# Feed-forward: where the two Silus of a part stand in ScalarE's queue

## The chip, the cores and the metric

The kernel runs on one core of a Trainium2 chip. A core has TensorE (PE) for matrix products, VectorE (DVE), ScalarE (ACT) and GpSimd (POOL) for work on tiles, and SyncE (SP), whose queue issues all the DMAs here. Each engine works through its own queue of instructions in order and waits by semaphores for the others. The metric is the device time of one execution in microseconds (us). A few runs of one kernel lie within about 0.2% of each other.

## The reference

Two sequences (one of 256 positions, one of 512, handled together as T = 768 columns) go through a trunk of two layers, each with a mixer (an mLSTM in layer 0, sliding-window attention in layer 1) and a feed-forward with a convolution. The change is in the feed-forward:

```
def conv_ffn(h, w_up, conv_w, conv_b, w_down):
    u = h @ w_up                                  # 1024 -> 2 * 2816
    u = depthwise_conv_width_3(u, conv_w) + conv_b
    g = u[..., :D_FF]
    val = u[..., D_FF:]
    return (jax.nn.silu(g) * val) @ w_down        # 2816 -> 1024
```

So each gate channel goes through the convolution and a Silu, and is multiplied by its value channel, before the down projection.

## The kernel before, in words

Channels lie on the 128 partitions and positions along the free dimension. All arithmetic is fp32. To multiply at speed, every fp32 operand is split into a rounded part ("hi", a cast on ScalarE, L236) and the remainder ("lo", a subtraction on VectorE, L237), and a product is made of three matmuls: hi x hi, lo x hi, hi x lo (L1275, L1276, L1277).

The 2816 gate channels and the 2816 value channels are cut into 11 **parts** of 256 and 256 (p = 0 to 10; the loop stands at the end of `ffn`). A part has two **pairs**: pair i = 0 makes the two blocks of 128 gate channels, pair i = 1 the two blocks of 128 value channels. `up(p)` makes both, then `down(p-1)` is written, so the down projection of one part stands behind the up projection of the next.

A pair multiplies by a scheme of Strassen's kind: seven products of quarter size instead of eight, called B11, B21, T1, T2, T3, T4 and B22 in the code, each of 12 matmuls (`quarters`). They accumulate in four fixed banks of PSUM, a, e, b and d. In the order in which `pair` writes them:

- B11 into a; ScalarE copies a to b (L1319, the **first copy**, or fork);
- T1 into e; ScalarE copies e to `p5` (L1324);
- T2 into b; ScalarE copies b to d (L1330, the **second copy**);
- B21 into a; ScalarE evicts a to the output row r1 (L1283 within `evict`);
- T3 into d; ScalarE copies d to `u3` (L1338, the **third copy**);
- B22 into b; VectorE makes the second half of r1 (L1340) and of r2 (L1341);
- T4 into d; ScalarE evicts d to r2.

The weights of a pair are loaded by SP, added up on POOL (L1303, L1306, L1307, L1315) and split on ScalarE and VectorE into buffers `whi` and `wlo`, three of each; a cast waits until PE has done with the buffer that it takes.

Behind each pair `up` writes the convolution of its two rows (`conv`): one step on ScalarE (L1499) and two on VectorE (L1501, L1502). For pair 0 each convolution is followed by a Silu on ScalarE in place (L1526). For pair 1 POOL multiplies the row by the gate's row (L1528) and the product is split for the down projection.

Part 0 is special: its two pairs are written out by hand in `head`, in an order that is kept as it is written on PE, ScalarE and VectorE (`manual_schedule`), and in part 1 the first pair lacks the two products that `head` has already made (`rest`), and both pairs' instructions are tied behind the end of `head` (`issue_after`).

Elsewhere the order of each engine's queue isn't the order of the text. When the kernel is built, a planner with a model of the instructions' times (`schedule_with_timeline_sim=True`) lays the instructions out: on each engine it issues what its model holds to be ready, earlier lines of the program first. The queues are fixed from then on. `issue_after(ins)` is a constraint for this planner: the instructions that a block writes on the engine of `ins` are issued behind `ins`. It adds no wait by a semaphore.

Of the kernel before, what the change touches and what calls it, by code (L numbers as in the profile page):

```python
# [12 lines left out]
AF = mybir.ActivationFunctionType  # L13
# [65 lines left out]
def col(t):  # L79

    return t + (GAP if t >= 256 else 0)
# [64 lines left out]
class Net:  # L146
# [1148 lines left out]
    def pair(self, pool, u, bank, rows, rest=False):  # L1295


        nc = self.nc
        r1, r2 = rows
        rb, ra = (self.load(u, h) for h in (1, 0))  # L1300
        q = [t[:, 512 * i : 512 * (i + 1)] for t in (ra, rb) for i in range(2)]
        tt = nc.gpsimd.tensor_tensor
        tt(q[2], q[2], q[3], ALU.add)  # L1303
        if not rest:
            wa = self.split(ra)
        tt(q[0], q[2], q[0], ALU.subtract)  # L1306
        tt(q[1], q[1], q[0], ALU.subtract)  # L1307
        s1h, s1l = (pool.tile([P, 512], R, tag=t, name=self.nm(t), bufs=1) for t in ("s1h", "s1l"))
        part = lambda w, i: [t[:, 512 * i : 512 * (i + 1)] for t in w]
        fork = r1[:, col(H) :]  # L1310
        if not rest:
            fork = a = bank(0)
            self.quarters(a, part(wa, 0), self.B11, True)
        self.fp_copy_split(s1h, s1l, q[2])
        tt(q[2], q[3], q[0], ALU.subtract)  # L1315
        wc = self.split(ra)
        wb = self.split(rb)
        e, b = bank(1), bank(2)
        nc.scalar.copy(b, fork)  # L1319
        p5 = self.tmp([P, H])  # L1320

        def fifth():
            self.quarters(e, (s1h, s1l), self.T1, True)
            nc.scalar.copy(p5, e)  # L1324

        if not rest:
            fifth()
        self.quarters(b, part(wc, 0), self.T2, False)
        d = bank(3)
        nc.scalar.copy(d, b)  # L1330
        if rest:
            fifth()
        else:
            self.quarters(a, part(wa, 1), self.B21, False)
            self.evict(r1, a)
        self.quarters(d, part(wb, 0), self.T3, False)
        u3 = self.tmp([P, H])
        nc.scalar.copy(u3, d)  # L1338
        self.quarters(b, part(wc, 1), self.B22, False)
        nc.vector.tensor_tensor(r1[:, col(H) :], b, p5, ALU.add)  # L1340
        nc.vector.tensor_tensor(r2[:, col(H) :], e, u3, ALU.add)  # L1341
        self.quarters(d, part(wb, 1), self.T4, False)
        self.evict(r2, d)

    def prepare(self, u0, l):

        flat = [z.rearrange("p j k t -> p (j k t)") for z in (self.zh, self.zl)]
        place = lambda j: [z[:, j : j + 1024] for z in flat]

        ahead = [place(12 * H), place(4 * H)]  # L1350
        wa = place(0)
        spare = None
        if l:

            spare = self.slab([P, 3072], R)
            wa = [spare[:, 1024 * (z + 1) : 1024 * (z + 2)] for z in range(2)]
        self.fp_copy_split(*wa, self.load(u0 + 1, 0))
        for i in range(0 if l else 2):
            self.fp_copy_split(*ahead[i], self.load(u0 + 3 + i, 0))
        return wa, ahead, spare  # L1360
# [123 lines left out]
    def ffn(self, l, xt, pool, last_tile, apply, keep=None):  # L1484
        nc = self.nc
        u0 = U_FFN + l * NPART * 3
        early = self.prepare(u0, l)
        next(last_tile)

        urows = [self.slab([P, 4, TG]) for _ in range(2)]  # L1490
        for urow in urows:
            nc.gpsimd.memset(urow[:, :, 256 : 256 + GAP], 0.0)

        behind = []

        def conv(u, y, ch):
            cb = self.cst(CB + l * 44 + ch)
            w = lambda tap: self.cst(CW + (l * 44 + ch) * 3 + tap)
            nc.scalar.activation(y, u, AF.Identity, bias=cb, scale=w(1))  # L1499
            stt = nc.vector.scalar_tensor_tensor  # L1500
            stt(y[:, 1:], u[:, :-1], w(0), y[:, 1:], ALU.mult, ALU.add)  # L1501
            stt(y[:, :-1], u[:, 1:], w(2), y[:, :-1], ALU.mult, ALU.add)  # L1502

        def up(p):
            urow = urows[0] if p == 0 else urows[1]
            fixed = lambda i: self.bank[i][:, :H]
            if p == 0:
                eng = mybir.EngineType
                self.ready(HALVES[0])
                with self.tc.manual_schedule(engines={eng.PE, eng.Activation, eng.DVE}):  # L1510
                    behind[:] = self.head(u0, last_tile, pool, urows, mark, early)
            for i in range(2):
                if p:
                    rows = [urow[:, 2 * i + j] for j in range(2)]
                    with ExitStack() as order:
                        for ins in behind[2 * i :] if p == 1 else ():
                            order.enter_context(self.tc.issue_after(ins))
                        self.pair(pool, u0 + 3 * p + i, fixed, rows, rest=p == 1)
                if i == 0:
                    yrow = self.slab([P, 4, TG])  # L1520
                    g = self.slab([P, 2, 2, TG], R)
                for j in range(2):
                    y = yrow[:, 2 * i + j]
                    conv(urow[:, 2 * i + j], y, i * FC + 2 * p + j)
                    if i == 0:
                        nc.scalar.activation(y, y, AF.Silu)  # L1526
                    else:
                        nc.gpsimd.tensor_tensor(y, y, yrow[:, j], ALU.mult)  # L1528
                        self.fp_copy_split(g[:, 0, j], g[:, 1, j], y)
            return g  # L1530

        def mark(t):

            hi, _ = self.quarter(self.B11)
            self.mm(t, hi[0][:, :P], hi[0], True, True)

        def down(p, g):
            ws = (w for _, w in self.halves(u0 + 3 * p + 2))
            chunk = lambda w, i: [t[:, 512 * i : 512 * (i + 1)] for t in w]

            def tile(w, c, rng):
                s0, s1, _ = rng
                o = self.pa()[:, : s1 - s0]
                cs = slice(c % 4 * P, (c % 4 + 1) * P)
                for i in range(2):
                    wh, wl = chunk(w, i)
                    gh, gl = (g[:, z, i, col(s0) : col(s0) + s1 - s0] for z in range(2))
                    self.mm(o, wh[:, cs], gh, i == 0, False)
                    self.mm(o, wh[:, cs], gl, False, False)
                    self.mm(o, wl[:, cs], gh, False, i == 1)  # L1550
                self.resid(xt, o, l, 40, c, rng)

            if p < NPART - 1:
                for h, w in enumerate(ws):
                    for rng in SAMPLE, PROMPT:
                        for c in range(4 * h, 4 * h + 4):
                            tile(w, c, rng)
                return
            ws = list(ws)
            for rng in RANGES:  # L1560
                norm = Norm(self, xt, rng, apply, last=keep is None and rng is RANGES[-1], adds=None if keep is not None else nc.vector)
                for c in range(KC):
                    tile(ws[c // 4], c, rng)
                    norm.square(c)
                    if keep is not None or rng is not RANGES[-1] or c < 3:
                        self.tick(0.65)
                if keep is not None:
                    self.save_x(xt, keep, rng)
                self.start(rng, norm.stages())

        prev = None
        for p in range(NPART):
            g = up(p)
            if prev is not None:
                down(*prev)
            prev = (p, g)
        down(*prev)
# [175 lines left out]
```

## Time and profile before

| | |
|---|---|
| median of 3 runs | 1882.17 us (1879.48 to 1883.78) |
| the profiled execution | 1885.06 us, its span 1883.3 us |
| PE busy | 1799.4 us |
| VectorE / ScalarE / POOL busy | 1412.1 / 912.2 / 488.7 us |
| Silus (L1526) | 44, of 848 ns (median) |
| the feed-forward's parts 1 to 10 | from about 555 us in layer 0 and from about 1373 us in layer 1 |

The span runs from the first to the last instruction. A row of a timeline gives the start in us from there, the length in us, the engine, the line of the kernel, the operation with the tile that it writes and those that it reads, and in brackets how long the engine stood idle before it and what ended that. "L1526" is line 1526 of the kernel before. Matmuls overlap: each is listed with about 0.33 us, but they start about 0.175 us apart.

### The profile page before, as it was taken

What the parts mean: (1) busy time and instruction counts of PE and PEld (TensorE: products, weight loads), DVE (VectorE), ACT (ScalarE), POOL (GpSimd) and SP (SyncE); (2) the same over time, 40 slices, a digit from 0 to 9 for tenths busy, and PEclk for the clock granted to TensorE, in tenths of its full rate; (3) what the DMA queues carried; (4) which work ended last, traced back from release to release, by engine and by line L of the source; (5) the groups of instructions that cost most, each with busy time, mean ns of one, the idle gap of its engine ahead of it and who ended that gap; (6) DMA issues with size and microseconds to landing.
All of it is one profiled execution on the core that took longest, in us unless ns stands there. A gap on an engine that the chain in (4) does not pass through costs nothing. (4 is left out here: it accounts for less than half of the span.)

```text
span 1883.3 us, 29169 instructions
## 1 busy us (share of the span) xinstructions
PE 1799.4 (96%) x11306; PEld 1659.1 (88%) x11306; DVE 1412.1 (75%) x2306; ACT 912.2 (48%) x1841; POOL 488.7 (26%) x390
## 2 busy tenths in 40 slices
PE   6989999999999999999999999989999999999997
PEld 5968887889988999999999988879989999999996
DVE  5866577685699777777777768865998777777777
ACT  4544334434464444444444557764564444444443
POOL 2010001021023333333332213330134333333322
PEclk9999999999999999999999999999999999999999
DMA  8354466556212122222223221312222222222211
GB/s 323 108 163 140 153 196 206 162 177 199 79 51 68 63 68 67 67 68 68 68 68 104 81 86 47 104 43 91 68 90 67 68 68 68 68 68 68 68 34 68
DMA packets 64246, 184.49 MB, mean 98 GB/s; under 512 B 6167, under 2 KB 23831, under 8 KB 64108
## 3 DMA queue, kind: packets, MB, share of 16 engines
q1 hardware_dynamic: 64108, 182.63, 30.0%
q8 instruction: 89, 1.46, 0.3%
q14 instruction: 49, 0.40, 0.1%
HBM read 176.17 MB, written 6.43 MB: 97 GB/s over the span
## 5 line engine op out<-in xcount | busy, mean ns | idle before, releaser
L236 ACT CAST whi<-raw 128x1024 fp32r<-128x1024 f32 x237 | 249.1, 1051 | 403.4 <-PE pa L230 197.4
L237 DVE TENSOR_TENSOR wlo<-raw,whi 128x1024 fp32r<-128x1024 f32 x237 | 331.1, 1397 | 113.9 <-ACT whi L236 108.5
L230 PE MATMUL pa<-slab,whi 128*128 128x256 f32 (+1 forms) x1472 | 347.3, 333 | 4.8 <-DVE slab L719 4.6
L230 PEld LDWEIGHTS pa<-slab,whi 128*128 128x128 f32 x1472 | 253.0, 190 | 31.8 <-DVE slab L719 6.3
L719 DVE SCALAR_TENSOR_TENSOR slab<-pa,mod,slab 128x256 f32<-128x256 f32 (+1 forms) x368 | 207.8, 592 | 70.8 <-PE pa L230 70.2
L230 PE MATMUL ps<-zh,whi 128*128 128x256 f32 (+2 forms) x688 | 232.5, 339 | 6.1 <-ACT whi L236 2.6
L230 PE MATMUL pa<-slab,wlo 128*128 128x256 f32 (+1 forms) x736 | 235.2, 331 | 0.0
L230 PE MATMUL ps<-zh,wlo 128*128 128x256 f32 (+2 forms) x688 | 227.0, 332 | 3.8 <-DVE wlo L237 3.8
L230 PE MATMUL ps<-zl,whi 128*128 128x256 f32 (+2 forms) x688 | 227.9, 332 | 1.4 <-DVE zl L539 0.9
L1275 PE MATMUL ps<-zh,whi 128*128 128x384 f32 x504 | 171.2, 340 | 16.7 <-ACT ps L1330 15.2
L1276 PE MATMUL ps<-zl,whi 128*128 128x384 f32 x504 | 169.8, 337 | 0.8 <-DVE zl L1233 0.8
L1277 PE MATMUL ps<-zh,wlo 128*128 128x384 f32 x504 | 169.1, 336 | 0.0
L230 PEld LDWEIGHTS pa<-slab,wlo 128*128 128x128 f32 x736 | 139.5, 190 | 13.0 <-DVE wlo L237 0.9
L230 PEld LDWEIGHTS ps<-zh,whi 128*128 128x128 f32 x688 | 131.0, 191 | 20.0 <-issue 3.5
L230 PEld LDWEIGHTS ps<-zh,wlo 128*128 128x128 f32 x688 | 131.2, 191 | 14.8 <-DVE wlo L237 4.8
L230 PEld LDWEIGHTS ps<-zl,whi 128*128 128x128 f32 x688 | 131.3, 191 | 10.4 <-DVE zl L539 1.1
L1528 POOL TENSOR_TENSOR slab<-slab 128x772 f32<-128x772 f32 x44 | 83.8, 1906 | 210.5 <-DVE slab L1502 199.1
L1306 POOL TENSOR_TENSOR raw<-raw,raw 128x512 f32<-128x512 f32 x40 | 52.3, 1308 | 293.9 <-DVE wlo L237 243.8
L1501 DVE SCALAR_TENSOR_TENSOR slab<-slab,cstt,slab 128x771 f32<-128x771 f32 x88 | 105.7, 1202 | 27.0 <-ACT slab L1499 27.0
L1502 DVE SCALAR_TENSOR_TENSOR slab<-slab,cstt,slab 128x771 f32<-128x771 f32 x88 | 120.2, 1366 | 0.8
L1275 PEld LDWEIGHTS ps<-zh,whi 128*128 128x128 f32 x504 | 94.6, 188 | 24.8 <-ACT ps L1330 20.4
L472 DVE SCALAR_TENSOR_TENSOR ada<-raw,silc,ada 128x1024 f32<-128x1024 f32 x84 | 111.6, 1360 | 2.3 <-DMA raw<-in_adaln_w_dram 2.3
(300 smaller groups left out, 4127.9 us busy)
## 6 DMA issues: line engine op xcount, KB each, us to landing
raw<-in_w_dram SPq DMA_DIRECT2D x208, 512.0 KB, 3.7
raw<-in_adaln_w_dram SPq DMA_DIRECT2D x84, 512.0 KB, 4.5
slab<-in_x_dram SPq DMA_DIRECT2D x12, 512.0 KB, 8.9
slab<-in_adaln_w_dram SPq DMA_DIRECT2D x12, 512.0 KB, 10.2
slab<-mrows SPq DMA_DIRECT2D x8, 384.0 KB, 5.4
xs<-slab SPq DMA_DIRECT2D x6, 512.0 KB, 2.9
bt<-brow SPq DMA_DIRECT2D x16, 192.0 KB, 3.3
slab<-xs SPq DMA_DIRECT2D x6, 512.0 KB, 5.7
```

The source lines that it names most:

```text
L230: self.last_mm = self.nc.tensor.matmul(out, lhsT, rhs, start=start, stop=stop)
L236: nc.scalar.copy(hi, src)
L237: return nc.vector.tensor_tensor(lo, src, hi.bitcast(F32), ALU.subtract)
L472: stt(acc[:, s], row, w, acc[:, s], ALU.mult, ALU.add)
L719: self.nc.vector.scalar_tensor_tensor(x, o, self.mod[l][:, gc + c, q : q + 1], x, ALU.mult, ALU.add)
L1275: mm(o, wh[:, k], hi[k], start=start and k == 0, stop=False, skip_group_check=True)
L1276: mm(o, wh[:, k], lo[k], start=False, stop=False, skip_group_check=True)
L1277: mm(o, wl[:, k], hi[k], start=False, stop=k == 3, skip_group_check=True)
L1306: tt(q[0], q[2], q[0], ALU.subtract)
L1501: stt(y[:, 1:], u[:, :-1], w(0), y[:, 1:], ALU.mult, ALU.add)
L1502: stt(y[:, :-1], u[:, 1:], w(2), y[:, :-1], ALU.mult, ALU.add)
L1528: nc.gpsimd.tensor_tensor(y, y, yrow[:, j], ALU.mult)
```

## The change

The two Silus of a part are no longer written behind the convolutions of the first pair. They are written ahead of the second pair's convolutions, and, in every part but part 0, tied behind the third copy of the second pair, which `pair` now returns. Part 0, whose pairs are made in `head`, has no such copy and gets no tie.

```diff
@@ pair
         u3 = self.tmp([P, H])
-        nc.scalar.copy(u3, d)
+        third = nc.scalar.copy(u3, d)
...
         self.quarters(d, part(wb, 1), self.T4, False)
         self.evict(r2, d)
+        return third.ins
@@ ffn, up
-                        self.pair(pool, u0 + 3 * p + i, fixed, rows, rest=p == 1)
+                        third = self.pair(pool, u0 + 3 * p + i, fixed, rows, rest=p == 1)
                 if i == 0:
                     yrow = self.slab([P, 4, TG])
                     g = self.slab([P, 2, 2, TG], R)
+                if i:
+                    with self.tc.issue_after(third) if p else ExitStack():
+                        for j in range(2):
+                            nc.scalar.activation(yrow[:, j], yrow[:, j], AF.Silu)
                 for j in range(2):
                     y = yrow[:, 2 * i + j]
                     conv(urow[:, 2 * i + j], y, i * FC + 2 * p + j)
-                    if i == 0:
-                        nc.scalar.activation(y, y, AF.Silu)
-                    else:
+                    if i:
                         nc.gpsimd.tensor_tensor(y, y, yrow[:, j], ALU.mult)
                         self.fp_copy_split(g[:, 0, j], g[:, 1, j], y)
```

## The prediction

> **What bounds the kernel now.** I read the page first: busy shares, the shares of the chain that ended last, and the costliest groups.
>
> ```profile
> span 1883.3 us, 29169 instructions
> ...
> PE 1799.4 (96%) x11306; PEld 1659.1 (88%) x11306; DVE 1412.1 (75%) x2306; ACT 912.2 (48%) x1841; POOL 488.7 (26%) x390
> ...
> L1275 PE MATMUL ps<-zh,whi 128*128 128x384 f32 x504 | 171.2, 340 | 16.7 <-ACT ps L1330 15.2
> ```
>
> PE is busy for 96% of the span, so in the feed-forward only a wait of PE itself can be worth time. Of the idle time in front of the feed-forward's matmuls, 15.2 us is put down to one ScalarE instruction, the second copy of a pair (L1330, which forks bank b into bank d). Next I asked for the waits of PE alone, in two windows. The first holds parts 2 to 9 of layer 0 and the start of part 10; the second, parts 2 to 10 of layer 1 from the end of part 2's first pair.
>
> ```profile
> PE ps L1275 <- ACT ps L1330: 5.6, 7, 0.9
> PE ps L1275 <- ACT ps L1319: 0.2, 1, 0.2
> ```
> ```profile
> PE ps L1275 <- ACT ps L1330: 7.1, 7, 1.9
> PE ps L1275 <- ACT ps L1319: 0.2, 1, 0.2
> ```
>
> The columns are microseconds in total, times, and the longest. In some 780 us PE waits for hardly anything else: 7 + 7 waits of 5.6 + 7.1 = 12.7 us, one in the second pair of each of parts 3 to 9. ScalarE's timeline in part 3 (bracket: idle time before the row, and what ended it) says why.
>
> ```profile
> 665.77 0.84 ACT L1526 ACTIVATE slab<-slab 128x772 f32<-128x772 f32 x1
> ...
> 669.75 0.47 ACT L1324 COPY nt<-ps 128x384 f32<-128x384 f32 x1
> 672.03 0.85 ACT L1526 ACTIVATE slab<-slab 128x772 f32<-128x772 f32 x1 [1.80 <-DVE slab L1502]
> 672.78 0.47 ACT L1330 COPY ps<-ps 128x384 f32<-128x384 f32 x1
> 673.19 1.04 ACT L236 CAST whi<-raw 128x1024 fp32r<-128x1024 f32 x1
> ...
> 675.69 0.48 ACT L1338 COPY nt<-ps 128x384 f32<-128x384 f32 x1 [1.03 <-PE ps L1277]
> 677.64 1.06 ACT L236 CAST whi<-raw 128x1024 fp32r<-128x1024 f32 x1 [1.46 <-PE ps L1276]
> 678.59 1.03 ACT L1499 ACTIVATE slab<-slab,cstt 128x772 f32<-128x772 f32 x1
> ```
>
> The second Silu (672.03) stands in ScalarE's queue ahead of L1330. It waits 1.80 us for the convolution's last VectorE step, runs, and only then does the copy go. PE at the same place:
>
> ```profile
> 671.81 0.33 PE L1277 MATMUL ps<-zh,wlo 128*128 128x384 f32 x1
> 671.98 0.34 PE L1276 MATMUL ps<-yl,whi 128*128 128x384 f32 x1
> 672.16 0.34 PE L1277 MATMUL ps<-yh,wlo 128*128 128x384 f32 x1
> 673.30 0.44 PE L1275 MATMUL ps<-zh,whi 128*128 128x384 f32 x1 [0.81 <-ACT ps L1330]
> 673.59 0.34 PE L1276 MATMUL ps<-zl,whi 128*128 128x384 f32 x1
> ```
>
> The row at 671.81 is the last matmul of T2 into bank b, on which L1330 depends. Only two matmuls of B21 are left as filler behind it; at 673.30 T3 begins, on the copied bank.
>
> **The change part by part.** *What is removed:* in parts 3 to 9 both Silus leave the queue ahead of L1330. It does not go to nothing, because L1330 still has to follow T2's last matmul. How quickly it can is seen where no Silu stands before it, in part 10 (ScalarE, then PE):
>
> ```profile
> 1002.37 0.46 ACT L1330 COPY ps<-ps 128x384 f32<-128x384 f32 x1 [1.88 <-PE ps L1277]
> ```
> ```profile
> 1002.00 0.33 PE L1277 MATMUL ps<-zh,wlo 128*128 128x384 f32 x1
> 1002.18 0.34 PE L1276 MATMUL ps<-yl,whi 128*128 128x384 f32 x1
> ...
> 1003.41 0.34 PE L1277 MATMUL ps<-yh,wlo 128*128 128x384 f32 x1
> 1003.59 0.34 PE L1275 MATMUL ps<-zh,whi 128*128 128x384 f32 x1
> ```
>
> The copy started 1002.37 - 1002.00 = 0.37 us after the start of T2's last matmul. There eight fillers followed (1002.18 to 1003.41) and PE did not wait. In part 3 T3 started 673.30 - 672.78 = 0.52 us after the copy. So T3 can start 0.37 + 0.52 = 0.89 us after T2's last matmul starts: 671.81 + 0.89 = 672.70 instead of 673.30. That is 0.60 of the 0.81 us; 0.21 us of idle time stays, since two fillers cover too little. L1324 ends at 670.22, ahead of the new start of 672.18, so nothing on ScalarE holds the copy.
>
> The sum over 14 parts: 12.7 us less 14 x 0.21 = 2.9 leaves **9.8 us**. This takes PE's order as it is. That is my choice between two ends. If the planner leaves no filler, T3 follows T2's last matmul by 0.89 against a modelled end of 0.34: idle 0.55, sum 12.7 - 14 x 0.55 = 5.0 us. If it leaves many fillers, as in part 10, the wait goes whole, and with it the restart: from 672.16 to 673.59 is 1.43 us for two steps of 0.18, so a stall of 0.81 costs 1.07, 0.27 us more than its idle time; the sum is 12.7 + 14 x 0.27 = 16.5 us. I take the middle because the fillers are spent while T2 waits for its weights, and no Silu feeds those.
>
> The Trainium skill (TensorE: Matmul & The Clock Gate, "Single matmul latency") gives a lone warm matmul of N columns (398 + N)/2.4 ns, so 326 ns for 384. No row here shows that latency alone; with 0.33 for the 0.37 above, an estimate by the page, the residue would be 0.17 us and the sum 10.3. The same section against its back-to-back gap of N/2.4 + 2.5 ns makes a restart 0.16 us; the rows show 0.27, and by the page the whole wait would be worth 15.0 us instead of 16.5.
>
> *What is added behind the third copy (L1338):* two Silus, in all 20 parts that have a second pair.
>
> ```profile
> L1526 ACT ACTIVATE slab<-slab x44: 833/848/860, 562.4 to 1821.7; 128x772 f32<-128x772 f32 x44
> ```
>
> Start to start a Silu takes 672.78 - 672.03 = 0.75 us, two 1.50. ScalarE is idle for 1.46 us after L1338, until PE frees a buffer for the weight cast at 677.64. The pair fills that gap and delays the cast and the convolution's L1499 behind it by 0.0 to 0.2 us. No semaphore wait is added: copy and Silus are on one engine, and the convolution that the second Silu reads ended by 672.03, where the old one started. The readers of the Silus are the products on POOL:
>
> ```profile
> 682.09 1.86 POOL L1528 TENSOR_TENSOR slab<-slab 128x772 f32<-128x772 f32 x1 [6.89 <-DVE slab L1502]
> ```
>
> The second Silu would end near 676.1 + 0.75 + 0.85 = 677.7, 4.4 us before the product, which is held by the second pair's own convolution. So I cost the additions at nothing; without that cover, 0.2 us a part, 4 us. The Silus pass the weight casts, evictions, L1499, L1324, L1330 and L1338 of ScalarE's queue. They issue no DMA and pass nothing on SP's or POOL's.
>
> *Parts that gain nothing:* in parts 1, 2 and 10 PE doesn't wait for a second pair's L1330. Part 0 has no third copy, so its Silus are not tied. There the table load stays, and with it a wait of part 1's first pair, once in each layer (ScalarE, then PE, in layer 0):
>
> ```profile
> 559.13 1.03 ACT L1499 ACTIVATE slab<-slab,cstt 128x772 f32<-128x772 f32 x1
> ...
> 561.07 1.28 ACT L1526 ACT_TABLE_LOAD   x1
> ```
> ```profile
> 565.02 0.44 PE L1275 MATMUL ps<-zh,whi 128*128 128x384 f32 x1 [1.30 <-ACT ps L1330]
> ```
>
> The two Silus of part 0 are now written behind both convolutions of its first pair instead of one each. Three of the part's four convolutions were issued ahead of the first Silu anyway (the third at 559.13), so I count 0.
>
> **The rivals.**
>
> *The wait goes whole.* With the Silus gone the planner lays T2 earlier against B21 and fillers cover L1330: 16.5 us, 1865.7. For it: parts 2 and 10, where PE doesn't wait. Against: there no Silu stood before T2 either way; part 10's extra fillers go with having no next pair whose weight sums run on POOL.
>
> *The down projection's cast takes the freed place (slower).* ScalarE now idles before L1330, and the cast behind it (673.19) needs only the buffer that B21 frees. If the planner's model has B21 done before T2, that cast is issued first. So it stands in the first pair of the same parts:
>
> ```profile
> 655.42 1.05 ACT L236 CAST whi<-raw 128x1024 fp32r<-128x1024 f32 x1 [7.85 <-PE pa L230]
> 656.38 0.47 ACT L1330 COPY ps<-ps 128x384 f32<-128x384 f32 x1
> ```
>
> Then the cast starts 0.37 after B21's last matmul (672.16), L1330 0.96 later, T3 0.52 after that: 674.01, an idle time of 1.51 us; 14 x 1.51 = 21.1 against 12.7, so 8.4 us slower, 1890.6. It decides from the point where T2 ends behind B21; now it ends two matmuls, 0.35 us, ahead.
>
> *No change.* The order is planned anew from the changed list, and 14 new waits of some 0.7 us come up elsewhere, or the Silus are issued still later and hold the casts. For it: PE already shows small waits of other kinds, like L1319's 0.2 us. Against: outside these 14 waits PE waits for nothing in the steady parts, so every other supply runs ahead of it. 1882.
>
> **How the numbers follow.** The profiled execution took 1885.06 us, 1.8 more than its span and 2.9 above the median of 1882.17; the saving is taken off the median: 1882.17 - 9.8 = **1872.4**. Chances: this case, with its ends of 5.0 and 16.5 left to the range, 0.64 (own range 1869 to 1878); whole wait gone 0.16; no change 0.11; slower 0.09. The range of 1865 to 1879 takes in the first two. A measurement of this kernel can tell about 0.2%, 3.8 us, from no change; the first two are beyond that but for some 0.02 at the small end, so faster 0.78, same 0.13, slower 0.09.
>
> **What would show it.** Right: both Silus directly behind L1338; L1330 released by PE in parts 3 to 9, 0.37 us behind T2's last matmul; PE's wait for it at 14 times 0.2 us, some 3 us; part 1's wait of 1.30 unchanged; a part of layer 0 shorter by some 0.6 us. Wrong: a weight cast between L1324 and L1330; other fillers than two; a wait of PE for L237, L719 or L1341 that wasn't there; POOL's product released by a Silu.

## The result, and the profile after

The kernel after the change took 1873.63 us (median of 5; 1870.02 to 1875.08), the kernel before 1882.17 (5 runs of the same session). The ratio is 0.9948 with a 95% interval of 0.9936 to 0.9959: 7.7 to 12.0 us faster, where 9.8 was forecast. Timed again beside the last experiments it was 0.9939 (0.9927 to 0.9951). Two executions were disturbed and stand in no ratio: the profiled one of B21 tied on the kernel after (2194.83 us at a granted clock of 0.751, so no lengths are read from it) and one of the twelve without the tie (6169.47 us).

The page of the profiled execution after the change (1875.08 us, 10.0 under that of before):

```profile
span 1873.0 us, 29153 instructions
...
PE 1801.3 (96%) x11306; PEld 1662.3 (89%) x11306; DVE 1400.9 (75%) x2306; ACT 911.0 (49%) x1841; POOL 497.9 (27%) x390
...
L1275 PE MATMUL ps<-zh,whi 128*128 128x384 f32 x504 | 171.0, 339 | 6.4 <-ACT ps L1330 5.4
```

Each engine's count of instructions is that of before. The idle time ahead of the feed-forward's matmuls that is put down to the second copy (L1330) fell from 15.2 to 5.4 us. PE's waits in the windows of parts 2 to 9 and on, layer 0 and then layer 1, were these and no others:

```profile
PE ps L1275 <- ACT ps L1330: 1.4, 7, 0.2
```
```profile
PE ps L1275 <- ACT ps L1330: 1.4, 7, 0.2
```

Seven and seven waits are still there, each of 0.2 us. ScalarE's timeline in part 3, for comparison with that of before (L1500 is the convolution's step now):

```profile
671.87 0.47 ACT L1324 COPY nt<-ps 128x384 f32<-128x384 f32 x1
674.33 0.46 ACT L1330 COPY ps<-ps 128x384 f32<-128x384 f32 x1 [1.99 <-PE ps L1277]
674.71 1.05 ACT L236 CAST whi<-raw 128x1024 fp32r<-128x1024 f32 x1
...
677.24 0.48 ACT L1338 COPY nt<-ps 128x384 f32<-128x384 f32 x1 [1.04 <-PE ps L1277]
677.62 1.59 ACT L1526 ACTIVATE slab<-slab 128x772 f32<-128x772 f32 x2
679.18 1.05 ACT L236 CAST whi<-raw 128x1024 fp32r<-128x1024 f32 x1
680.14 1.03 ACT L1500 ACTIVATE slab<-slab,cstt 128x772 f32<-128x772 f32 x1
```

The bracket at L1330 now names PE where a Silu stood, both Silus (x2) run right behind L1338, and the weight cast at 679.18 follows them without a gap. PE at the same place:

```profile
673.96 0.33 PE L1277 MATMUL ps<-zh,wlo 128*128 128x384 f32 x1
674.14 0.34 PE L1276 MATMUL ps<-yl,whi 128*128 128x384 f32 x1
674.31 0.34 PE L1277 MATMUL ps<-yh,wlo 128*128 128x384 f32 x1
674.85 0.45 PE L1275 MATMUL ps<-zh,whi 128*128 128x384 f32 x1 [0.20 <-ACT ps L1330]
```

T2's last matmul, the same two fillers, then T3 0.89 us after the start of T2's last matmul.

For the sum over parts I use a length that agreed to 0.02 us in all profiles with the same order of queues: from the second copy of part 3's first pair to that of part 10's. Its ends in layer 0, before and after:

```profile
656.38 0.47 ACT L1330 COPY ps<-ps 128x384 f32<-128x384 f32 x1
...
987.63 0.47 ACT L1330 COPY ps<-ps 128x384 f32<-128x384 f32 x1
```
```profile
658.53 0.47 ACT L1330 COPY ps<-ps 128x384 f32<-128x384 f32 x1
...
985.51 0.47 ACT L1330 COPY ps<-ps 128x384 f32<-128x384 f32 x1
```

So seven parts took 331.25 us before and 326.98 after; in layer 1, read in the same way, 332.44 and 326.77. Together that is 9.94 us. The rest of the span's 10.3 us nearly cancels: the stretch ahead of part 1 is 2.15 us longer, that between the layers 1.65 shorter, the end 0.86 shorter, parts 1 and 2 equal to 0.02 in both layers. At the end, behind the feed-forward, one wait of PE for VectorE (L112) is 0.25 us instead of 1.13, which was not forecast. The other pieces vary between two profiles of one kernel: the second profile of the kernel after came to part 1 2.28 us earlier than the first, took 0.88 us longer between the layers, and was 1.5 us shorter in parts 1 and 2 of layer 1 (90.28 us), where two waits of 0.9 and 0.5 us are missing. So it is partly luck that the whole gain, too, came out near 9.8.

### The profile page after: what moved, and what is told of

Read it like the earlier page. It is cut to its first block, busy times and chain, and to the rows that moved or that the text cites. A ratio compares the mean times of both kernels' runs of the same rounds, so it can differ in the third digit from the quotient of the medians.

```text
span 1873.0 us, 29153 instructions
## 1 busy us (share of the span) xinstructions
PE 1801.3 (96%) x11306; PEld 1662.3 (89%) x11306; DVE 1400.9 (75%) x2306; ACT 911.0 (49%) x1841; POOL 497.9 (27%) x390
## 3 DMA queue, kind: packets, MB, share of 16 engines
q8 instruction: 89, 1.46, 0.3%
## 5 line engine op out<-in xcount | busy, mean ns | idle before, releaser
L237 DVE TENSOR_TENSOR wlo<-raw,whi 128x1024 fp32r<-128x1024 f32 x237 | 316.3, 1335 | 108.8 <-ACT whi L236 107.7
L719 DVE SCALAR_TENSOR_TENSOR slab<-pa,mod,slab 128x256 f32<-128x256 f32 (+1 forms) x368 | 207.5, 591 | 70.9 <-PE pa L230 70.6
L230 PEld LDWEIGHTS ps<-zh,whi 128*128 128x128 f32 x688 | 132.2, 192 | 20.3 <-issue 3.5
L1503 DVE SCALAR_TENSOR_TENSOR slab<-slab,cstt,slab 128x771 f32<-128x771 f32 x88 | 120.1, 1365 | 0.8
L1303 POOL TENSOR_TENSOR raw<-raw 128x512 f32<-128x512 f32 x40 | 64.8, 1619 | 186.1 <-DMA raw<-in_w_dram 178.4
## 6 DMA issues: line engine op xcount, KB each, us to landing
slab<-in_adaln_w_dram SPq DMA_DIRECT2D x12, 512.0 KB, 10.3
```

Of the source, the lines that this page charges most:

```text
L230: self.last_mm = self.nc.tensor.matmul(out, lhsT, rhs, start=start, stop=stop)
L237: return nc.vector.tensor_tensor(lo, src, hi.bitcast(F32), ALU.subtract)
L719: self.nc.vector.scalar_tensor_tensor(x, o, self.mod[l][:, gc + c, q : q + 1], x, ALU.mult, ALU.add)
```

## The experiments

All ratios are to the kernel before, timed beside the run on the same chip. The table gives the length from part 3 to part 10 in both layers from the profile of each.

| run | median us | ratio (95% interval) | parts 3 to 9, layers 0 and 1 |
|---|---|---|---|
| before | 1882.17 | | 331.25, 332.44 |
| after | 1873.63 | 0.9948 (0.9936 to 0.9959) | 326.98, 326.77 |
| only the second Silu tied | 1870.58 | 0.9941 (0.9928 to 0.9955) | 326.98, 326.77 |
| only the first Silu tied | 1883.26 | 1.0010 (1.0001 to 1.0019) | 331.54, 331.57 |
| no tie | 1881.04 | 0.9995 (0.9986 to 1.0004) | 331.23, 331.30 |
| tie behind the second copy | 1869.83 | 0.9939 (0.9923 to 0.9956) | 326.01, 325.91 |
| after, B21 behind T2 | 1868.55 | 0.9935 (0.9923 to 0.9948) | not read |
| before, B21 behind T2 | 1866.34 | 0.9925 (0.9911 to 0.9939) | 323.51, 323.56 |
| after, table load early | 1869.83 | 0.9951 (0.9938 to 0.9964) | 326.98, 326.77 |
| after, part 1 as before | 1870.70 | 0.9950 (0.9938 to 0.9962) | 326.98, 326.77 |
| after, two more behind | 1896.45 | 1.0069 (1.0055 to 1.0083) | 335.96, 336.09 |
| before, B21 behind T2, tie in part 1 | 1868.92 | 0.9921 (0.9909 to 0.9934) | 323.51, 323.56 |
| after, the same two ties | 1868.95 | 0.9927 (0.9915 to 0.9940) | 323.87, 323.83 |
| after, again | 1871.98 | 0.9939 (0.9927 to 0.9951) | 326.98, 326.77 |

**Which Silu.** Only one of the two is tied behind the third copy, the other stands behind its own convolution as before.

```diff
-                        for j in range(2):
+                        for j in (1,):          # the other run: (0,)
                             nc.scalar.activation(yrow[:, j], yrow[:, j], AF.Silu)
...
                     conv(urow[:, 2 * i + j], y, i * FC + 2 * p + j)
+                    if i == 0 and j == 0:       # the other run: j == 1
+                        nc.scalar.activation(y, y, AF.Silu)
```

Expected of the second alone:

> The first gate row's Silu is back behind its convolution, untied; only the second row's Silu is tied behind the third copy. Theory A (only the Silu that waits 1.80 us for VectorE in front of the second copy costs time): parts 3 to 9 as after the change, PE's wait for the second copy 14 x 0.20 us, some 9 us faster than before, 1873. Theory B (each Silu taken out from between the two copies gives half, since ScalarE has less to do there): some 5 us faster, 1877.

Expected of the first alone:

> The reverse: the first gate row's Silu is tied behind the third copy, the second row's stands behind its convolution as before, and so again ahead of the second copy in parts 3 to 9. Theory A: PE's wait for the second copy stays at 14 times 0.7 to 1.9 us, 12 us or more in total, time within 2 us of before, 1882. Theory B: some 5 us faster, 1877.

PE's waits for the second copy in parts 3 to 9 of layer 0, the second Silu tied and then the first:

```profile
PE ps L1275 <- ACT ps L1330: 1.4, 7, 0.2
```
```profile
PE ps L1275 <- ACT ps L1330: 6.0, 7, 1.4
```

The second Silu is the whole of it: its tie alone gives the lengths of the change to the hundredth, the first's gives nothing (if anything 0.1% more time). It isn't ScalarE's load between the copies that counted, but one instruction that waited there.

**Is the tie needed?**

```diff
-                    with self.tc.issue_after(third) if p else ExitStack():
+                    with ExitStack():
```

> Both Silus stay where the change writes them, but the tie behind the third copy is left out. Theory A (the tie does it): the planner, which takes what it holds to be ready, issues the second Silu ahead of the second copy again in the steady parts; PE's wait for the copy 12 to 13 us, time as before, 1882. Rival (it is enough to write the Silus later): as after the change, 1873.

Written late but free, the second Silu came ahead of the copy again in the steady parts, with the wait of before (ScalarE, part 4):

```profile
721.50 0.85 ACT L1526 ACTIVATE slab<-slab 128x772 f32<-128x772 f32 x1 [1.80 <-DVE slab L1503]
722.25 0.47 ACT L1330 COPY ps<-ps 128x384 f32<-128x384 f32 x1
```

The interval of the ratio, 0.9986 to 1.0004, takes in 1. The place in the text alone does nothing in the steady parts; the planner takes what its model holds to be ready.

**A tie behind the second copy.**

```diff
-        nc.scalar.copy(d, b)
+        third = nc.scalar.copy(d, b)
         if rest:
...
-        third = nc.scalar.copy(u3, d)
+        nc.scalar.copy(u3, d)
```

> The tie is behind the second copy (bank b to d) instead of the third, so both Silus run right behind it and ahead of the weight cast, the eviction of r1 and the third copy. Theory A: the second copy is as free as after the change, PE's wait for it 14 x 0.20 us; two Silus (1.5), cast (1.0) and eviction (0.5) then need 3.4 us behind the copy where the third copy is due 2.9 us after it, so the third copy comes about 0.5 us late, which VectorE's slack takes up: some 9 us faster than before, 1873. Rival (the place behind the third copy, with its 1.46 us of idle time, is what keeps the gain): the late cast or third copy makes new waits of PE of some 0.5 us in each of 14 to 18 parts, and 2 us or less of the gain is left, 1880 or more.

It is as good, and its parts are 0.9 us a layer shorter. ScalarE in part 4, then PE:

```profile
720.24 0.46 ACT L1330 COPY ps<-ps 128x384 f32<-128x384 f32 x1 [0.88 <-PE ps L1277]
720.61 1.59 ACT L1526 ACTIVATE slab<-slab 128x772 f32<-128x772 f32 x2
722.10 1.04 ACT L236 CAST whi<-raw 128x1024 fp32r<-128x1024 f32 x1
723.03 0.54 ACT L1283 COPY slab<-ps 128x128 f32<-128x128 f32 x2
723.45 0.50 ACT L1338 COPY nt<-ps 128x384 f32<-128x384 f32 x1
```
```profile
719.86 0.33 PE L1277 MATMUL ps<-zh,wlo 128*128 128x384 f32 x1
720.04 0.34 PE L1277 MATMUL ps<-yh,wlo 128*128 128x384 f32 x1
...
720.57 0.34 PE L1277 MATMUL ps<-yh,wlo 128*128 128x384 f32 x1
720.75 0.44 PE L1275 MATMUL ps<-zh,whi 128*128 128x384 f32 x1
```

L1338 comes without an idle time ahead of it, so it is late, as expected, and PE didn't mind. The planner laid four fillers here instead of two (720.04 to 720.57), and PE waits for the copy in one part of each layer only. So the place behind the third copy isn't what keeps the gain.

**The two fillers.** B21's matmuls are tied behind T2's last one, on the kernel after and on the kernel before (`quarters` returns its last matmul).

```diff
-        self.quarters(b, part(wc, 0), self.T2, False)
+        t2 = self.quarters(b, part(wc, 0), self.T2, False)
...
-            self.quarters(a, part(wa, 1), self.B21, False)
+            with self.tc.issue_after(t2.ins):
+                self.quarters(a, part(wa, 1), self.B21, False)
```

> The change, and besides B21's twelve matmuls of the ordinary pairs are tied behind T2's last matmul, so that twelve of them, not two, stand between T2 and T3. Theory A (what is left of the wait, 14 x 0.20 us of idle time and 14 x 0.27 us of restart, comes from only two fillers covering the 0.89 us from T2's last matmul to T3): PE's wait for the second copy goes to nothing, some 6.5 us faster than after the change, 1867. Rival (T2 was put behind B21's matmuls because its weights come late, so without fillers ahead of it T2 waits instead): PE waits for the split of T2's weights on VectorE, 0.3 us or more in each of the 14 parts, and the time is that of after the change or slower, 1873 to 1878.

> The kernel before, Silus in their old place in the text, with the same tie of B21 behind T2. The planner then issues the second copy ahead of the second Silu by itself. Theory A (any way that lets the second copy go 1 us or more before T3 gives the same): PE's wait for the second copy goes to nothing in parts 3 to 9, 16 us faster than before, 1866, as fast as the change with this tie. Rival (the Silus behind the third copy are needed for it): the second Silu, now right behind the second copy, holds the weight cast and the third copy instead, and 5 us or more of that are lost, 1871 or more.

The first has no lengths, and its time decides little: the ratio of 0.9935 makes 1869.9 of 1882.17, midway between the two theories' 1867 and 1873. On the same chip it is 0.0015, 2.8 us, under the two other versions of the change (0.9951 and 0.9950), where 6.5 were expected. A later run with the same tie (below) took 323.87 and 323.83 us in parts 3 to 9, 6 less than the change. The second is clear. PE and ScalarE in part 4:

```profile
716.28 0.33 PE L1277 MATMUL ps<-zh,wlo 128*128 128x384 f32 x1
716.46 0.34 PE L1275 MATMUL ps<-yh,whi 128*128 128x384 f32 x1
...
718.40 0.34 PE L1277 MATMUL ps<-yh,wlo 128*128 128x384 f32 x1
718.58 0.34 PE L1275 MATMUL ps<-zh,whi 128*128 128x384 f32 x1
```
```profile
716.65 0.46 ACT L1331 COPY ps<-ps 128x384 f32<-128x384 f32 x1 [0.29 <-PE ps L1277]
718.16 0.85 ACT L1528 ACTIVATE slab<-slab 128x772 f32<-128x772 f32 x1 [1.04 <-DVE slab L1504]
```

Twelve fillers cover the copy, the old Silu goes behind the copy by itself, and PE waits for nothing in parts 3 to 9 of either layer. They take 323.51 + 323.56 us, 16.6 less than before: the 16.5 that the prediction gave for the whole wait with its restarts. T2 did not run short of weights.

**The table load.** A Silu of two zeros is put into part 0's opening.

```diff
         nc.scalar.copy(d2, b2)
+        zero = self.silc[:, 0, 2:4]
+        nc.scalar.activation(zero, zero, AF.Silu)
         low()
```

> The change, with a Silu of two columns of zeros in part 0's opening, so that the table load of 1.28 us runs there, where ScalarE idles for 2.04 us, and not ahead of part 0's first Silu. Theory A (part 1's first wait of 1.28 us, once a layer, is the table load's): this wait goes from 1.28 to 0.3 us or less in both layers, 2 to 3 us faster than after the change, 1871. Rival (T2 there ends late anyway, and the casts and evictions behind the Silu hold the copy): the wait stays above 0.9 us, time as after the change, 1873.

ScalarE, and PE in part 1:

```profile
547.47 1.28 ACT L1464 ACT_TABLE_LOAD   x1
...
566.84 1.05 ACT L236 CAST whi<-raw 128x1024 fp32r<-128x1024 f32 x1 [1.52 <-PE pa L1276]
567.79 0.53 ACT L1283 COPY slab<-pa 128x128 f32<-128x128 f32 x2
568.21 0.49 ACT L1330 COPY ps<-ps 128x384 f32<-128x384 f32 x1
```
```profile
568.76 0.44 PE L1275 MATMUL ps<-zh,whi 128*128 128x384 f32 x1 [1.26 <-ACT ps L1330]
```

Theory A fell: the load is out of the way and the wait is as long as ever. What stands ahead of the copy is a weight cast that waits 1.52 us for its buffer, and two evictions. Not all of the wait can be theirs: the last matmul of T2 starts at 567.16 and no filler follows it (both pairs of part 1, not only the first, are written with `rest` and have no B21), so by the 0.89 us of the steady parts some 0.55 us of idle time would stay without them. That is an estimate; no run took them away without another wait in their place.

**Part 1.** In the profile after, one wait of PE within the down projection that stands behind part 1's pairs had doubled; before, it was 0.87:

```profile
607.75 0.51 PE L230 MATMUL pa<-slab,whi 128*128 128x256 f32 x2 [1.70 <-DVE slab L719]
```

So part 1's Silus were put back alone.

```diff
-                if i:
+                if i and p != 1:
                     with self.tc.issue_after(third) if p else ExitStack():
...
                     conv(urow[:, 2 * i + j], y, i * FC + 2 * p + j)
+                    if i == 0 and p == 1:
+                        nc.scalar.activation(y, y, AF.Silu)
```

> The change for parts 2 to 10 only; part 1 has its Silus in the old place. After the change PE's wait for VectorE's residual step at the start of part 1's down projection grew from 0.87 to 1.70 us in layer 0 and from 0.86 to 1.68 in layer 1. Theory A (the later Silus of part 1 push VectorE's work there): that wait goes back to 0.87, the wait for the first copy of 0.2 us in part 2 comes back, and the sum is within 1 us of after the change, 1873. Rival (it is a wait that the change adds for nothing): 1.6 us faster than after the change, 1872.

The wait went back to 0.85 us in layer 0 and 0.87 in layer 1; the wait for the first copy in part 2 came back in layer 1 only. The forecasts, 1873 and 1872, lie too close for the ratio, which is that of the change (0.9950), so the lengths decide: parts 1 and 2 took 91.51 and 91.89 us against 91.90 and 91.80, 0.3 us less in all where the rival had 1.6. Most of what the longer wait costs is gained beside it.

**The cover behind the third copy.**

```diff
+                if i and p:
+                    with self.tc.issue_after(third):
+                        for j in range(2):
+                            nc.scalar.activation(yrow[:, j], yrow[:, j], AF.Copy)
```

> The change, and behind the two Silus two more ScalarE instructions of the same size (each gate row copied onto itself), also tied behind the third copy. The planner lays one of them ahead of the weight cast and one behind it, so the cast comes some 0.7 us and the second pair's convolution some 1.5 us later than after the change. Theory A (what stands behind the third copy is off PE's path, with more cover than the 1.46 us of ScalarE's idle time): time within 2 us of after the change, PE's waits unchanged. Rival (the cover is those 1.46 us and no more): each part is longer by 0.7 to 1.5 us, 14 to 30 us in all, 1887 to 1903.

My theory fell: the run is 14 us slower than before and 24.5 slower than the change beside it, with a new wait in each of parts 2 to 9 of both layers (the ninth wait is part 1's old one). PE's longest waits in layer 0, from the opening to part 9:

```profile
PE pa L230 <- DVE slab L719: 8.7, 9, 1.0
```

ScalarE, then VectorE and PE, in this run's part 4:

```profile
723.59 0.48 ACT L1338 COPY nt<-ps 128x384 f32<-128x384 f32 x1 [1.04 <-PE ps L1277]
...
727.88 1.02 ACT L1500 ACTIVATE slab<-slab,cstt 128x772 f32<-128x772 f32 x1
```
```profile
739.94 1.01 DVE L1503 SCALAR_TENSOR_TENSOR slab<-slab,cstt,slab 128x771 f32<-128x771 f32 x1
740.87 1.65 DVE L719 SCALAR_TENSOR_TENSOR slab<-pa,mod,slab 128x256 f32<-128x256 f32 x4
```
```profile
741.40 0.73 PE L230 MATMUL pa<-slab,whi 128*128 128x512 f32 x2 [0.97 <-DVE slab L719]
```

After the change, VectorE and PE in part 3:

```profile
690.73 2.04 DVE L1503 SCALAR_TENSOR_TENSOR slab<-slab,cstt,slab 128x771 f32<-128x771 f32 x1
692.69 1.64 DVE L719 SCALAR_TENSOR_TENSOR slab<-pa,mod,slab 128x256 f32<-128x256 f32 x4
```
```profile
693.88 0.62 PE L230 MATMUL pa<-slab,whi 128*128 128x512 f32 x2
```

The second pair's convolution steps (L1503) stand in VectorE's queue ahead of the residual steps (L719) that empty PE's banks for the down projection. After the change the first of the four L719 takes about 0.48 us, as single ones of its size do, and ends some 0.7 us before PE takes its bank at 693.88. That is the cover at this place, and it lies on VectorE. With the convolution's ScalarE step 4.29 us behind the third copy (727.88 - 723.59) instead of 2.90 (680.14 - 677.24), this L719 starts 17.28 us behind it instead of 15.45; of the 1.83 us, 0.7 are covered, and PE waits 0.97. A part gets 1.28 us longer ((335.96 - 326.98) / 7).

But the 1.83 us are not simply the lateness handed on, since VectorE's order was planned anew. The split of `s1` (the weights of T1) stood behind the four L719 after the change; in the run with two more it stands ahead of L1503 and of them:

```profile
694.26 1.07 DVE L237 TENSOR_TENSOR s1l<-raw,s1h 128x512 fp32r<-128x512 f32 x1
```
```profile
738.24 1.78 DVE L237 TENSOR_TENSOR s1l<-raw,s1h 128x512 fp32r<-128x512 f32 x1
```

By the rows, the lateness was 1.17 us at the first convolution step, 0.31 at the first L719 behind it (VectorE had idled there for 0.78 us), 1.16 again behind a weight split that took 2.50 us instead of 1.63, and 1.83 behind the split of `s1` (1.70 us more, less 1.03 by which L1503 ran shorter). So the run shows that more work behind the third copy reaches PE through VectorE's queue; how much of the 1.28 us is the delay itself and how much the new order, no run separates.

**Towards a faster version.** With B21 tied, part 1's second pair was tied on ScalarE behind its first pair's second copy, on the kernel before and after.

```diff
-        nc.scalar.copy(d, b)
+        second = nc.scalar.copy(d, b)
         if rest:
+            if len(self.ahead) < 3:
+                self.ahead.append(second.ins)
...
+                        self.ahead = behind
                         for ins in behind[2 * i :] if p == 1 else ():
```

> The kernel before with B21 tied behind T2, and besides in part 1 the second pair's ScalarE instructions tied behind the first pair's second copy, so that no weight cast that waits for its buffer goes ahead of that copy. Theory A (part 1's first wait of 1.3 us is a cast's, not the table load's): that wait goes to 0.3 us or less in both layers, with its restart 2 to 3 us faster than without the second tie, 1863 to 1865. Rival (something else in part 1 is next by as much): PE's waits in part 1 move and sum to the same, no change, 1866.

> The same two ties on the kernel after the change. Theory A (once B21 covers the second copy the Silus' place no longer matters): parts 3 to 9 last as long as with the old Silus and the tie, 323.5 us a layer, and the time is that of the run with the old Silus within 2 us. Rival (the Silus behind the third copy are worth something of their own): 3 us or more faster than that run.

> The kernel after the change once more, beside the three others on the same chip: 0.995 of before, 1873, parts 3 to 9 of 327.0 and 326.8 us.

The tie in part 1 failed: it took the cast away and the planner put another waiting instruction there, the split of a product that waits for POOL. ScalarE and PE with the old Silus:

```profile
565.41 0.84 ACT L236 CAST slab<-slab 128x772 fp32r<-128x772 f32 x1 [1.65 <-POOL slab L1533]
566.15 0.47 ACT L1331 COPY ps<-ps 128x384 f32<-128x384 f32 x1
```
```profile
566.67 0.69 PE L1275 MATMUL ps<-zh,whi 128*128 128x384 f32 x1 [2.97 <-ACT ps L1331]
```

The wait grew from 1.3 to 3.0 us, and parts 1 and 2 together took as long as without the tie (181.8 us over both layers against 181.6, lengths that vary by 1.5 us a layer from profile to profile). Behind this wait PE also ran slower: from 566.67 to 569.72 its matmuls start 0.32 us apart instead of 0.175, at a granted clock of 0.50, and so in layer 1. With B21 tied the place of the Silus no longer matters: 1868.92 and 1868.95 us. On the same chip the change alone took 1871.98, so the better version is some 3 us faster than it, though parts 3 to 9 are 6 us shorter. 1.5 us of the difference are given back from part 10's first second copy to the end of the span, where the profile with both ties and the new Silus shows 77.3 us against 75.8: PE's wait for L112, behind the feed-forward, is 1.69 us there and 0.24 with the change alone. The rest is within what the pieces ahead of the parts vary by. The intervals of the ratios, 0.9915 to 0.9940 and 0.9927 to 0.9951, overlap, so the 3 us are a rough figure.

## Why the prediction was right

*The wait and its cause.* Right: a Silu that waits for VectorE, ahead of the second copy in ScalarE's queue. The prediction spoke of both Silus leaving; the runs with one of them show that the second alone did it.

*The residue.* Right to the hundredth: T3 at T2's last matmul plus 0.89 us, the forecast 0.21 us of idle time in each of 14 parts measured as 0.20, 2.8 us in all, since PE's order kept its two fillers. The saving in these parts is 9.94 us against 9.8. The estimate from the Trainium skill's latency of a single bf16 matmul (TensorE: Matmul & The Clock Gate, "Single matmul latency"), 10.3, was worse: the copy again started 674.33 - 673.96 = 0.37 us behind the start of the matmul, as in part 10 before, not 0.33. For the restart too the rows were the better guide: with the whole wait gone parts 3 to 9 were 16.6 us shorter, near the rows' 16.5, not the 15.0 estimated from the Trainium skill's two formulas (the same page, "Single matmul latency" and "Back-to-back issue gap").

*The ends that were weighed.* More fillers did appear, but with other edits: four by the tie behind the second copy, twelve by the tie on PE. The rival that named this expected it of the Silus' leaving alone; with the tie behind the third copy the order kept its two fillers, and only the tie on PE took the wait away in every part.

*The slower rival.* It didn't come, but its mechanism exists: in part 1 a weight cast and two evictions stand ahead of the second copy, before and after, and PE waits 1.3 us there.

*The step that failed, without harm to the sum:* "There the table load stays, and with it a wait of part 1's first pair". The load stays, but with the load out of the way the wait was still 1.26 us.

*The step that was too light:* "without that cover, 0.2 us a part, 4 us". The additions cost nothing, as said: the weight cast comes 1.94 us and the convolution's step 2.90 us behind the third copy, where they came 1.95 and 2.90 before. But the cover that I named, ScalarE's 1.46 us ahead of the cast, is not the last one: behind it VectorE's queue has some 0.7 us at its L719, and it is there that PE came to wait. The price without cover is not bounded by 0.2 us a part: it was 1.28 with two more instructions, in an order planned anew.

*Part 1's longer wait* for L719 (0.87 to 1.70 us) was not forecast; all but some 0.3 us of it cancels within parts 1 and 2.

## What to carry to other kernels

In an in-order queue look for the instruction that waits just ahead of one that the bound engine needs; moving the one that waits was worth the bound engine's wait here, moving the other was worth nothing. Price the gain to the next dependence, not to zero: here the copy still had to follow its product, and the remaining 0.2 us and the restart went when more independent matmuls stood between the two. Where you move work to, follow its successors through the next in-order queue: an engine that idles 1.5 us at that place can feed one with less slack, and a planner may lay out that one's queue anew.

## What the runs showed of the hardware that I had not expected

A wait of PE cost 0.28 us more than its listed idle time: over 14 waits of 12.7 us in all, removal gave 16.6. The rows of the kernel before show two pieces of it. The idle time is counted from the modelled end of the last matmul, 0.34 us after its start, where the next would have started 0.175 us after it: 0.16 us. And behind the first matmul after a wait the next starts 0.29 us later (673.30 to 673.59), not 0.175: 0.11 us.

A longer wait cost more than that: behind the wait of 2.97 us PE's granted clock was 0.50 for some 3 us, in both layers and with the old and the new Silus, while behind the waits of 0.7 to 1.9 us in parts 3 to 9 of the kernel before it stayed at 1.00. What makes the clock fall the runs do not show.

And the 1.28 us of an activation table load could be moved by 13 us without any effect on a wait that it seemed to cause; the cast behind it waited for its buffer instead.
